# Second layer's experts: weights in 8 KB runs, and four experts as one unit

## The chip, the cores and the metric

One core of a Trainium2 chip runs the whole program. The metric is the device time of one execution in microseconds (us). TensorE (PE) does the matmuls, with its weight loads shown apart (PEld); VectorE (DVE), ScalarE (ACT) and GpSimd (POOL) work beside it; SyncE (SP) issues nearly all transfers from memory (HBM) into the on-chip buffer, which 16 DMA engines carry out.

## The reference, cut to what matters

Two layers, each a mixer followed by a mixture of experts. The change touches the second layer's mixture alone, which sees 256 tokens of 1024 floats:

```python
def grouped_moe(h, router_w, router_b, w_gate, w_up, w_down):
    ...   # each token goes to 2 of 16 experts, both in its best group of four
    for e in range(N_EXPERTS):
        hid = jax.nn.silu(h @ w_gate[e]) * (h @ w_up[e])     # 1024 -> 512
        out = out + combine[:, e:e + 1] * (hid @ w_down[e])  # 512 -> 1024
    return out
```

All weights are float32. One expert has three matrices of 2 MiB (gate and up 1024 x 512, down 512 x 1024), so a layer's experts are 96 MiB.

## The kernel before, in words

**Units.** A layer's experts are worked off in units. A unit of one expert ("S") has 128 slots for tokens, a unit of two ("P") 64 slots for each; `PLAN` (L24) gives the order, for layer two `PPSPSPPPP`. Experts 0 to 4 stand at fixed places (units 0 to 2), so that their weights can be loaded before the routing is known. The others are sorted by their number of tokens (`order`): the fullest is the later S, the next ones fill the pairs from the fullest down, so the emptiest four are the last two pairs. Their numbers reach SyncE as register values (`expert`, L293). If an expert has more tokens than slots, a fallback (`overflow`) runs all experts for the tokens that found no slot.

**One unit.** Its token numbers come from a comparison of ranks (`slots1`), GpSimd gathers the token rows (`gather1`, three units ahead), TensorE transposes them in 8 blocks of 128 x 128 (`xpose1`, L1628) so that the features lie on partitions, block k holding features 128k to 128k+127. `gu` computes gate and up with the tokens as weight operand and the experts' matrices streamed past them. `hidden` makes silu(gate) x up x routing weight, `hid_T` transposes it in 4 blocks, `down` multiplies with the down matrix, first the left half of the output, then the right half, and splits each half into a high and a low part. `combine1` adds the result to the tokens' rows by a one-hot matmul. In program order these stand as gate n+1, down n, up n+1, combine n; a scheduler orders each engine's instructions at build time from its own model of durations.

**Matmuls.** `mm_unit` (L906) goes through the four blocks of a tile. For an S unit each product is three float32r matmuls of high and low parts (`mm3`), whose parts ScalarE, VectorE and GpSimd make per tile. For a P unit each expert's matmul is plain float32 on half of TensorE's columns (64), the two experts one after the other for each block; in the profile a float32 matmul stands as two records.

**Weights.** `Stream` (L95) holds the list of all weight tiles of the program in the order of use: for layer two gate 0, up 0, gate 1, down 0, up 1, and so on (`add_moe`, L301). A tile is 128 partitions x 4 x 512 floats, 1 MiB. A free buffer is filled with the next tile of the list by SyncE (`load`, L127); when the last matmul of a tile is issued, its buffer is released and the next load goes behind it. In layer two there are 12 buffers: `RING` = 7, `EXTRA` = 4, and one made of two separate halves (`Two`), which takes two transfers. Every tile is read as 512 rows x 512 columns, row 128k + p on partition p at place k: each partition gets four runs of 512 floats, 2 KB each. For the down matrix a tile is a column half.

**The end.** The last unit's down has its own code: product, weighting, one-hot matmul, addition and the squares for the final norm for the left half, then for the right half; then the test for overflow, the norm and two output transfers of 512 KB.

Of the kernel before, what the change touches and what calls it, by code (L numbers as in the profile page):

```python
# [10 lines left out]
F32 = mybir.dt.float32  # L11
# [3 lines left out]
OP = mybir.AluOpType  # L15
AX = mybir.AxisListType

D = 1024
KD = 8
NE = 16  # L20
EPS = 1e-6
NEG = -1.0e30
OFF = 4096.0
PLAN = ("SSSPSSSPSSSPS", "PPSPSPPPP")  # L24
FIXED = (2, 5)

RING, NPIECE = 7, 4
# [11 lines left out]

C_TRI, C_ONE, C_IOR, C_END = 0, 128, 256, 384  # L40

C_IOP, C_IDT, C_RK, C_THR, C_IO2, C_EID, C_KBE, C_KB, C_CAP, C_SEL, C_SEND = 0, 1, 5, 9, 13, 14, 15, 17, 49, 81, 97


def units_of(l):

    plan, fixed = PLAN[l], FIXED[l]
    units, p = [], 0
    while p < fixed:
        n = 1 + (plan[len(units)] == "P")  # L50
        units.append(tuple(range(p, p + n)))
        p += n
    rest = plan[len(units):]
    solo, pairs = iter(range(p, NE)), iter(range(p + rest.count("S"), NE, 2))
    for x in rest:
        if x == "S":
            units.append((next(solo),))
        else:
            p = next(pairs)
            units.append((p, p + 1))  # L60
    return units


# [35 lines left out]
class Stream:  # L99
# [28 lines left out]
    def load(self):  # L128
        while self.free and self.loaded < min(len(self.src), self.limit):
            i = self.loaded  # L130
            self.owner[i] = self.free.pop(0)
            t = self.owner[i][0]()
            for dst, src in self.src[i]:
                src = src() if callable(src) else src
                if isinstance(t, Two):
                    for j in range(2):
                        self.nc.sync.dma_start(t.t[j], src[:, 2 * j:2 * j + 2])
                elif i in self.behind:
                    with self.tc.issue_after(self.behind[i].ins):
                        self.nc.gpsimd.dma_start(dst(t), src)  # L140
                else:
                    self.nc.sync.dma_start(dst(t), src)
            self.tiles[i] = t
            self.loaded += 1
# [63 lines left out]
def backbone(ctx: ExitStack, tc: tile.TileContext, I, out):  # L208
# [16 lines left out]
    def y_t():  # L225
        return psum.tile([128, 512], F32, name="yp", tag="yp", bufs=2)
# [5 lines left out]
    st = Stream(tc, ring, RING, NPIECE)  # L232
# [67 lines left out]
    def add_moe(l):  # L300
        def src(w, p, r0, c0):  # L301
            return [(lambda t: t, lambda: w[expert(l, p), r0:r0 + 512, c0:c0 + 512].rearrange(
                "a (k p) f -> (a p) k f", p=128))]

        def put(name, w, u, pos):
            for r0, c0 in pos:
                for p in u:
                    st.add((name, l, p), src(w, p, r0, c0), len(u) == 1)

        wg, wu, wd = (I[n][l] for n in ("moe_w_gate", "moe_w_up", "moe_w_down"))  # L310
        rows2, cols2 = ((0, 0), (512, 0)), ((0, 0), (0, 512))
        for n, u in enumerate(UNITS[l]):
            put("g", wg, u, rows2)
            if n:
                put("d", wd, UNITS[l][n - 1], cols2)
            put("u", wu, u, rows2)
        put("d", wd, UNITS[l][-1], cols2)

    add_moe(0)
    for p in ADA_ODD[:NPRE]:  # L320
# [52 lines left out]
    rk4 = csm[:, C_RK:C_RK + 4]  # L373
    thr = csm[:, C_THR:C_THR + 4]
    iop2 = csm[:, C_IO2:C_IO2 + 1]
    eid = csm[:, C_EID:C_EID + 1]
    kbe = [csm[0:16, C_KBE + l:C_KBE + l + 1] for l in range(2)]
    kb = [csm[0:16, C_KB + 16 * l:C_KB + 16 * l + 16] for l in range(2)]
# [528 lines left out]
    def mm_unit(o, l, n, name, xh, xl, s, first, last, between=()):  # L907

        u = UNITS[l][n]
        w = [st.take((name, l, p)) for p in u]  # L910
        i = st.taken - len(u)
        for k in range(4):
            kk = s * 4 + k
            if len(u) == 1:
                mm3(o, xh[:, kk], xl[:, kk], w[0].h(k), w[0].l(k), first and k == 0, last and k == 3)
            else:
                for h in range(2):
                    hs = slice(h * 64, h * 64 + 64)
                    T.matmul(o[hs], xh[:, kk, hs].bitcast(F32), w[h][:, k], start=first and k == 0, stop=last and k == 3,  # L919
                             skip_group_check=True)  # L920
            if k == 1 and len(u) == 1:
                st.half()
            if k == 3:
                for h in range(len(u)):
                    st.done(i + h)
            if k % 2:
                for f in between[k // 2:k // 2 + 1]:
                    f()

    def gu(name, l, n, xh, xl, at={}):  # L930
# [6 lines left out]
            mm_unit(pp, l, n, name, xh, xl, s, s == 0, s == 1, [run(at.get(s * 2 + j, ())) for j in range(2)])  # L937
        return pp

    def down(pool, l, n, hh, hl, yh, yl):  # L940
        for half in range(2):
            pp = y_t()
            mm_unit(pp, l, n, "d", hh, hl, 0, True, True)
            hs = slice(half * 512, half * 512 + 512)
            split(yh[:, hs], yl[:, hs], pp, V)

    def order(l, pool, nch, oh):

# [50 lines left out]
    def spread_ranks(u, rT, n):  # L999

        m = 128 // len(u)
        pb = tr_t()
        if len(u) == 1:
            T.matmul(pb[:, 0:n], idr[:, u[0]:u[0] + 1].to_broadcast([16, 128]), rT, start=True, stop=True)
        else:
            for h in range(2):
                T.matmul(pb[h * m:h * m + m, 0:n], idt[0:16, u[h]:u[h] + 1].to_broadcast([16, m]), rT.bitcast(F32),
                         start=True, stop=True, skip_group_check=True)
        return pb[:, 0:n], iop if len(u) == 1 else iop2

    def hidden(pool, pg, pu, w):
        sg = pool.tile([128, 512], F32, name="sg", tag="sg", bufs=2)
# [1 line left out]
        V.scalar_tensor_tensor(sg, sg, w, pu, op0=OP.mult, op1=OP.mult)  # L1014
        return sg

    def hid_T(pool, hid, pair):
        pt = tr_t()
        for q in range(4):
            T.transpose(pt[:, q * 128:(q + 1) * 128], hid[:, q * 128:(q + 1) * 128], idt)  # L1020
        hh = pool.tile([128, 4, 128], F32R, name="hh", tag="hh", bufs=1)
        if pair:
            V.tensor_copy(hh.bitcast(F32).rearrange("p k t -> p (k t)"), pt)  # L1023
            return hh, None
        hl = pool.tile([128, 4, 128], F32R, name="hl", tag="hl", bufs=1)
        p4 = pt.rearrange("p (k t) -> p k t", k=4)
        S.activation(hh, p4, AF.Copy)
        V.tensor_sub(hl, p4, hh.bitcast(F32))
        return hh, hl
# [550 lines left out]
    with phase("moe1") as mp:  # L1580
# [18 lines left out]
        def slots1(n):  # L1599

            u = units[n]
            w = 128 // len(u)
            sg = mp.tile([128, 2, 128], F32, name="sgm", tag="sgm", bufs=2)
            for c in range(2):
                for h, p in enumerate(u):
                    V.tensor_scalar(sg[:, c, h * w:h * w + w], ior[:, 0:w], ranks[:, c, p:p + 1], None, op0=OP.is_equal)
            pw_ = tr_t()
            m = 2 * len(u)
            for c in range(2):
                T.matmul(pw_[:, 0:m], sg[:, c], idw[:, c, u[0]:u[0] + len(u)].rearrange("p e j -> p (e j)"),  # L1610
                         start=(c == 0), stop=(c == 1))
            V.tensor_scalar(sli[0:w, n:n + 1], pw_[0:w, 1:2], OFF, None, op0=OP.add)
            if len(u) == 2:
                V.tensor_scalar(sli[w:128, n:n + 1], pw_[w:128, 3:4], OFF, None, op0=OP.add)
            t = mp.tile([128, 1], F32, name="slw1", tag="slw1", bufs=4)
            for h in range(len(u)):
                hs = slice(h * w, h * w + w)
                V.tensor_copy(t[hs], pw_[hs, 2 * h:2 * h + 1])
            slw[n] = t
            return sg  # L1620
# [7 lines left out]
        def xpose1(n, sg=None):  # L1628
# [3 lines left out]
            for hf in range(2):  # L1632
                pt = tr_t()
                for q in range(4):
                    ks = slice((hf * 4 + q) * 128, (hf * 4 + q) * 128 + 128)
                    o = pt[:, q * 128:(q + 1) * 128]
                    if sg is None:
                        T.transpose(o, xg[n][:, ks], idt)
                    else:
                        for c in range(2):  # L1640
                            T.matmul(o, f1[c][:, ks], sg[:, c], start=(c == 0), stop=(c == 1))
                fs = slice(hf * 4, hf * 4 + 4)
                if xl is None:
                    (V.tensor_copy if hf else S.copy)(xh[:, fs].bitcast(F32).rearrange("p k t -> p (k t)"), pt)
                else:
                    split(xh[:, fs], xl[:, fs], pt.rearrange("p (k t) -> p k t", k=4), V)
# [38 lines left out]
        reg = any_over(mp, over)  # L1685
        for n in range(NU):
            if n:
                down1(n - 1, *hid_T(mp, hid, len(units[n - 1]) == 2))
            pu = gu("u", 1, n, *xT[n])
            hid = hidden(mp, pg, pu, slw[n])  # L1690
            slotsT1(n)
# [6 lines left out]
                    gather1(n + 3)  # L1698
                pg = gu("g", 1, n + 1, *xT[n + 1])

        hh, hl = hid_T(mp, hid, len(units[-1]) == 2)
        gfb = mp.tile([128, D], F32, name="gfb", tag="xl", bufs=1)
        Q.dma_start(gfb, I["final_g"].partition_broadcast(128))
        yb = x_t("yb", "Y")
# [35 lines left out]
def constants():  # L1740
# [14 lines left out]
    small[:, C_RK:C_RK + 4] = 4 - np.arange(4)  # L1755
    small[:, C_THR:C_THR + 4] = 2 - np.arange(4)
    small[:, C_IO2] = p % 64 + 1
    small[:, C_EID] = p
    e = np.arange(NE)
    for l in range(2):  # L1760
# [62 lines left out]
```

## Time and profile before

| | |
|---|---|
| median of 3 runs | 1020.47 us (1019.87 to 1021.63) |
| the profiled execution | 1022.2 us |
| its span, first to last instruction | 1020.4 us |
| TensorE busy, mean granted clock | 943.5 us (92%), 0.963 |
| DVE, ACT, POOL busy | 538.9, 342.2, 351.0 us |
| HBM read | 295.97 MB, 294 GB/s over the span |

The profile is of one execution. Times in its rows count from the first instruction. "Busy" is the union of an engine's instructions; a matmul's end is modelled. A bracket behind an instruction is the engine's idle time before it and what ended that.

### The profile page before, as it was taken

What the parts mean: (1) busy time and instruction counts of PE and PEld (TensorE: products, weight loads), DVE (VectorE), ACT (ScalarE), POOL (GpSimd) and SP (SyncE); (2) the same over time, 40 slices, a digit from 0 to 9 for tenths busy, and PEclk for the clock granted to TensorE, in tenths of its full rate; (3) what the DMA queues carried; (4) which work ended last, traced back from release to release, by engine and by line L of the source; (5) the groups of instructions that cost most, each with busy time, mean ns of one, the idle gap of its engine ahead of it and who ended that gap; (6) DMA issues with size and microseconds to landing.
All of it is one profiled execution on the core that took longest, in us unless ns stands there. A gap on an engine that the chain in (4) does not pass through costs nothing. (4 is left out here: it accounts for less than half of the span.)

```text
span 1020.4 us, 12766 instructions
## 1 busy us (share of the span) xinstructions
PE 943.5 (92%) x4686; PEld 589.3 (58%) x4686; DVE 538.9 (53%) x931; ACT 342.2 (34%) x492; POOL 351.0 (34%) x244
## 2 busy tenths in 40 slices
PE   4999999988899999999999798999796999999995
PEld 2677677746675678558756577466553444643331
DVE  3552425286783777457935683648523464532223
ACT  3421113144563266236534362433201132410001
POOL 2351103235552746524823533023001242443112
PEclk9999999998899999999999999899985999999998
DMA  9964668948699799799599772495496899999993
GB/s 311 363 241 145 213 254 296 350 166 291 217 320 375 248 344 356 251 359 387 203 385 384 255 266 86 123 335 182 157 346 250 326 387 383 387 382 386 386 386 130
DMA packets 149316, 296.28 MB, mean 290 GB/s; under 512 B 6776, under 2 KB 17032, under 8 KB 149112
## 3 DMA queue, kind: packets, MB, share of 16 engines
q1 hardware_dynamic: 143080, 278.06, 76.3%
q0 software_dynamic: 6128, 17.26, 4.6%
q8 instruction: 40, 0.66, 0.3%
q14 instruction: 36, 0.29, 0.1%
q10 hardware_dynamic: 32, 0.01, 0.0%
HBM read 295.97 MB, written 4.24 MB: 294 GB/s over the span
## 5 line engine op out<-in xcount | busy, mean ns | idle before, releaser
L171 ACT ACTIVATE whi<-w 128x1024 fp32r<-128x1024 f32 x182 | 190.6, 1058 | 225.8 <-PE mm L506 93.2
L175 POOL TENSOR_TENSOR wlo<-w,whi 128x1024 fp32r<-128x1024 f32 x64 | 163.5, 2555 | 260.7 <-ACT whi L171 218.4
L175 DVE TENSOR_TENSOR wlo<-w,whi 128x1024 fp32r<-128x1024 f32 x118 | 178.4, 1524 | 95.8 <-ACT whi L171 94.9
L919 PE MATMUL mm<-w,xh 128*64 128x512 f32 x632 | 162.9, 607 | 0.5 <-DMA w<-in_moe_w_up_dram 0.5
L515 POOL TENSOR_TENSOR H<-H,am 128x512 f32<-128x512 f32 x68 | 95.6, 1423 | 146.9 <-DVE am L514 144.5
L919 PEld LDWEIGHTS mm<-w,xh 128*64 128x64 f32 x632 | 48.7, 139 | 90.9 <-issue 87.4
L504 PE MATMUL mm<-whi,xh 128*128 128x512 f32 x192 | 79.6, 414 | 2.4 <-DVE am L514 1.6
L505 PE MATMUL mm<-wlo,xh 128*128 128x512 f32 x192 | 78.8, 410 | 2.7 <-DVE wlo L175 2.3
L506 PE MATMUL mm<-whi,xl 128*128 128x512 f32 x192 | 78.0, 406 | 0.0
L919 PE MATMUL yp<-w,hh 128*64 128x512 f32 x288 | 74.0, 606 | 0.8 <-DVE hh L1023 0.8
L514 DVE TENSOR_TENSOR am<-mm,m5b 128x512 f32<-128x512 f32 x68 | 45.7, 684 | 30.6 <-PE mm L1221 19.5
L1221 PE MATMUL mm<-y,seT 128*128 128x512 f32 x208 | 54.5, 397 | 0.2 <-ACT y L509 0.2
L504 PE MATMUL mm<-aTh,whi 128*128 128x512 f32 x128 | 52.4, 416 | 2.1 <-ACT aTh L665 2.1
L505 PE MATMUL mm<-aTl,whi 128*128 128x512 f32 x128 | 51.7, 404 | 0.0
L506 PE MATMUL mm<-aTh,wlo 128*128 128x512 f32 x128 | 51.3, 402 | 0.0
L1221 PEld LDWEIGHTS mm<-y,seT 128*128 128x128 f32 x208 | 38.1, 188 | 15.4 <-issue 4.9
L919 PEld LDWEIGHTS yp<-w,hh 128*64 128x64 f32 x288 | 23.0, 140 | 41.0 <-issue 39.4
L504 PEld LDWEIGHTS mm<-whi,xh 128*128 128x128 f32 x192 | 37.4, 195 | 14.6 <-issue 4.7
L505 PEld LDWEIGHTS mm<-wlo,xh 128*128 128x128 f32 x192 | 37.5, 195 | 14.4 <-DVE wlo L175 3.4
L432 PE MATMUL yp<-w,sT 128*32 128x512 f32 x288 | 45.2, 642 | 0.0
L506 PEld LDWEIGHTS mm<-whi,xl 128*128 128x128 f32 x192 | 37.5, 195 | 7.8 <-DVE xl L510 0.3
L510 DVE TENSOR_TENSOR yl<-yp,yh 128x512 fp32r<-128x512 f32 x16 | 11.0, 690 | 58.4 <-ACT yh L509 58.4
(362 smaller groups left out, 1546.3 us busy)
## 6 DMA issues: line engine op xcount, KB each, us to landing
w<-in_moe_w_gate_dram SPq DMA_DIRECT2D x61, 1024.0 KB
w<-in_moe_w_up_dram SPq DMA_DIRECT2D x58, 1024.0 KB
w<-in_moe_w_down_dram SPq DMA_DIRECT2D x57, 1024.0 KB
w<-in_ada_w_dram SPq DMA_DIRECT2D x48, 1024.0 KB
w<-in_even_w_in_dram SPq DMA_DIRECT2D x8, 1024.0 KB
w<-in_odd_w_in_dram SPq DMA_DIRECT2D x5, 1024.0 KB
w<-in_even_w_out_dram SPq DMA_DIRECT2D x4, 1024.0 KB
s4b<-mrow SPq DMA_DIRECT2D x6, 512.0 KB
```

The source lines that it names most:

```text
L171: self.nc.scalar.activation(hi, t, AF.Copy)
L175: eng.tensor_sub(lo, t, hi.bitcast(F32))
L432: T.matmul(pa[32 * j:32 * j + 32, :], s_at(s * 4 + j, u), t[:, j, :], start=first and s == 0, stop=last and s == 1, skip_group_check=True)
L504: T.matmul(o, lh, rh, start=first, stop=False)
L505: T.matmul(o, lh, rl, start=False, stop=False)
L506: T.matmul(o, ll, rh, start=False, stop=last)
L510: eng.tensor_sub(lo, x, hi.bitcast(F32))
L514: V.tensor_mul(t, pp, m)
L515: eng.tensor_add(acc, acc, t)
L919: T.matmul(o[hs], xh[:, kk, hs].bitcast(F32), w[h][:, k], start=first and k == 0, stop=last and k == 3, skip_group_check=True)
L1221: marks["comb"] = T.matmul(pp, seT[n][:, c * 128:(c + 1) * 128], t[:, hs], start=(i == 0), stop=(i == 2 * len(ns) - 1))
```

## The change

Three things change, all in layer two (`l == 1`); layer one keeps its tiles, its units and its order.

1. A tile of gate or up holds rows 8p + 4s to 8p + 4s + 3 on partition p (s = 0 or 1), a tile of down rows 4p + 2s and 4p + 2s + 1 in full: 2048 floats that lie together in memory, a run of 8 KB a partition. The last unit's down keeps its column halves. A load into the buffer of two halves takes 4 KB runs.
2. So that tokens and hidden values meet these rows, the transposes read every eighth feature of the tokens (a step of 32 bytes) and every fourth of the hidden product (16 bytes). `down` takes both output halves from each tile, so it accumulates in its two banks side by side (`mm_down`).
3. The plan becomes `PPSPSPPQ`: the last two pairs are one unit "Q" of four experts with 32 slots each, on a quarter of TensorE's columns each.

```diff
-PLAN = ("SSSPSSSPSSSPS", "PPSPSPPPP")
+PLAN = ("SSSPSSSPSSSPS", "PPSPSPPQ")
+
+WIDE = {"S": 1, "P": 2, "Q": 4}
...
+                        if len(src.shape) == 2:
+                            self.nc.sync.dma_start(t.t[j].rearrange("p k f -> p (k f)"), src[:, 1024 * j:1024 * j + 1024])
+                        else:
+                            self.nc.sync.dma_start(t.t[j], src[:, 2 * j:2 * j + 2])
...
+        def rows_of(w, p, s):
+
+            return [(flat, lambda: w[expert(l, p)].rearrange("a (p s j) f -> s (a p) (j f)", p=128, s=2)[s])]
...
-                    st.add((name, l, p), src(w, p, r0, c0), len(u) == 1)
+                    st.add((name, l, p), src(w, p, r0, c0) if l == 0 or last else rows_of(w, p, s), len(u) == 1)
...
-        put("d", wd, UNITS[l][-1], cols2)
+        put("d", wd, UNITS[l][-1], cols2, True)
...
-                for h in range(2):
-                    hs = slice(h * 64, h * 64 + 64)
+                m = 128 // len(u)
+                for h in range(len(u)):
+                    hs = slice(h * m, h * m + m)
...
+    def mm_down(os, l, n, hh, hl, s):
+
+        u = UNITS[l][n]
+        w = [st.take(("d", l, p)) for p in u]
+        i = st.taken - len(u)
+        for k in range(4):
+            j, o = 2 * s + k // 2, os[k % 2]
+            if len(u) == 1:
+                mm3(o, hh[:, j], hl[:, j], w[0].h(k), w[0].l(k), j == 0, j == 3)
+            else:
+                m = 128 // len(u)
+                for h in range(len(u)):
+                    hs = slice(h * m, h * m + m)
+                    T.matmul(o[hs], hh[:, j, hs].bitcast(F32), w[h][:, k], start=j == 0, stop=j == 3,
+                             skip_group_check=True)
...
     def down(pool, l, n, hh, hl, yh, yl):
+        os = [y_t(), y_t()]
+        if l:
+            for s in range(2):
+                mm_down(os, l, n, hh, hl, s)
         for half in range(2):
-            pp = y_t()
-            mm_unit(pp, l, n, "d", hh, hl, 0, True, True)
             hs = slice(half * 512, half * 512 + 512)
-            split(yh[:, hs], yl[:, hs], pp, V)
+            if not l:
+                mm_unit(os[half], l, n, "d", hh, hl, 0, True, True)
+            split(yh[:, hs], yl[:, hs], os[half], V)
...
-            T.transpose(pt[:, q * 128:(q + 1) * 128], hid[:, q * 128:(q + 1) * 128], idt)
+
+            T.transpose(pt[:, q * 128:(q + 1) * 128], hid[:, q:512:4] if rows else hid[:, q * 128:(q + 1) * 128], idt)
...
-                    ks = slice((hf * 4 + q) * 128, (hf * 4 + q) * 128 + 128)
+
+                    ks = slice(hf * 4 + q, D, 8)
```

## Rows read from the trace of the kernel before

**Rows 1.** The page: span, busy time, transfer rate in 40 slices, packets.
```profile
span 1020.4 us, 12766 instructions
...
PE 943.5 (92%) x4686; PEld 589.3 (58%) x4686; DVE 538.9 (53%) x931; ACT 342.2 (34%) x492; POOL 351.0 (34%) x244
...
GB/s 311 363 241 145 213 254 296 350 166 291 217 320 375 248 344 356 251 359 387 203 385 384 255 266 86 123 335 182 157 346 250 326 387 383 387 382 386 386 386 130
DMA packets 149316, 296.28 MB, mean 290 GB/s; under 512 B 6776, under 2 KB 17032, under 8 KB 149112
```
**Rows 2.** Stretches of 20 us in layer two's experts, columns in the first line.
```profile
core 0: us, PE busy (x) PEld busy (x) DVE busy (x) ACT busy (x) POOL busy (x), PEclk, DMA share, GB/s
...
780.00:800.00 20.00, 17.61 (x68) 6.57 (x70) 7.52 (x13) 4.94 (x6) 3.35 (x2) 0.78 0.48 171
...
820.00:840.00 20.00, 18.43 (x81) 9.88 (x83) 11.75 (x17) 8.02 (x9) 5.54 (x4) 0.91 1.05 388
840.00:860.00 20.00, 20.00 (x91) 9.15 (x88) 7.05 (x12) 3.57 (x5) 5.57 (x5) 1.00 1.05 388
...
1000.00:1020.00 20.00, 10.04 (x38) 3.37 (x34) 6.84 (x10) 4.04 (x9) 5.10 (x5) 0.85 0.17 68
```
**Rows 3.** Waits of TensorE, 783 to 1003 us: us in total, times, longest.
```profile
PE mm L505 <- DVE wlo L175: 2.3, 1, 2.3
...
PE tr L1638 <- DVE hh L1023: 0.2, 1, 0.2
```
**Rows 4.** Timeline of SyncE's last weight issues: start, us, what, how many.
```profile
968.90 10.27 SPq L142 DMA_DIRECT2D w<-in_moe_w_up_dram  x4
979.41 11.85 SPq L142 DMA_DIRECT2D w<-in_moe_w_down_dram  x4
```
**Rows 5.** Timeline of the end: last down, last scaling of the output.
```profile
999.32 7.09 PE L919 MATMUL yp<-w,hh 128*64 128x512 f32 x32 [0.78 <-DVE hh L1023]
...
1015.57 1.15 ACT L1734 ACTIVATE hg<-hg,rs 128x1024 f32<-128x1024 f32 x1 [3.91 <-POOL rs L1732]
```
**Rows 6.** Two longer stretches of layer two's experts.
```profile
801.70:944.40 142.70, 137.93 (x619) 70.13 (x617) 68.57 (x104) 35.72 (x47) 54.52 (x36) 0.98 1.04 385
944.40:1000.80 56.40, 53.48 (x244) 19.08 (x244) 13.87 (x21) 4.26 (x8) 9.96 (x8) 1.00 1.04 384
```
**Rows 7.** A stretch in which the pooling bands' 8 KB rows are loaded.
```profile
591.50:592.50 1.00, 1.00 (x9) 0.95 (x10) 0.19 (x2) 1.00 (x2) 0.90 (x1) 1.00 1.00 426
```
**Rows 8.** Timeline of TensorE in a pair's down.
```profile
984.12 0.59 PE L919 MATMUL yp<-w,hh 128*64 128x512 f32 x1
984.13 0.59 PE L919 MATMUL yp<-wa,hh 128*64 128x512 f32 x1
984.55 0.59 PE L919 MATMUL yp<-w,hh 128*64 128x512 f32 x1
```
**Rows 9.** Timeline of TensorE, matmuls on 32 columns (the modulation's).
```profile
707.04 1.07 PE L432 MATMUL mm<-w,sT 128*32 128x512 f32 x8
```
**Rows 10.** Timeline of VectorE: hidden products of units 1, 6, 7, 8.
```profile
801.70 0.75 DVE L1014 SCALAR_TENSOR_TENSOR sg<-sg,slw,mm 128x512 f32<-128x512 f32 x1 [4.68 <-PE mm L919]
...
944.37 0.75 DVE L1014 SCALAR_TENSOR_TENSOR sg<-sg,slw,mm 128x512 f32<-128x512 f32 x1 [2.86 <-PE mm L919]
...
971.38 0.75 DVE L1014 SCALAR_TENSOR_TENSOR sg<-sg,slw,mm 128x512 f32<-128x512 f32 x1 [4.52 <-PE mm L919]
...
997.08 0.75 DVE L1014 SCALAR_TENSOR_TENSOR sg<-sg,slw,mm 128x512 f32<-128x512 f32 x1 [4.50 <-PE mm L919]
```
**Rows 11.** Timeline of TensorE: unit 7's token transposes and gate.
```profile
946.61 1.10 PE L1638 MATMUL tr<-idt,xg 128*128 128x128 f32 x8 [0.21 <-DVE hh L1023]
947.64 6.65 PE L919 MATMUL mm<-w,xh 128*64 128x512 f32 x29
```
**Rows 12.** Weight loads of transposes by line: ns min/median/max, first and last start.
```profile
L1638 PEld LDWEIGHTS tr<-idt,xg x64: 138/140/229, 777.5 to 947.3; 128*128 128x128 f32 x64
...
L480 PEld LDWEIGHTS tr<-idt,mcol x7: 85/88/102, 161.6 to 736.1; 128*8 128x8 f32 x4, 128*24 128x24 f32 x2, 128*16 128x16 f32 x1
```

## What the change does to the time, predicted

> **What bounds the kernel now.** I read the page first, then the table of stretches, then the waits of TensorE and the issues of SyncE, last the timeline of the end. The page shows TensorE busy for 92% of the span, and in the strip the transfers flat at 382 to 388 GB/s over the last slices but one [rows 1]. The stretches place this: in 780 to 800 us the transfers move 171 GB/s, between 800 and 1000 us DMA stands at its ceiling, and in the last one the transfers stop while some 20 us of work remain [rows 2]. That last stretch moves 68 GB/s x 20 us = 1.36 MB; two output writes of 0.52 MB are 1.05 of it, so 0.31 MB of weights are left at 1000 us and the last ones land near 1000.8 us.
>
> TensorE looks no less full. Between 783 and 1003 us its waits, seven rows from 2.3 down to 0.2 us, sum to 7.4 us, and none is for a transfer [rows 3]. So the matmuls are never late for weights, yet SyncE's late issues last 2.6 to 3 us each, which is the time of one tile: its queue is full [rows 4]. Both resources end together: DMA at 1000.8, the last down projection from 999.3 to 1006.4, and 14.0 us of combination, norm and output to 1020.4 [rows 5]. To shorten one alone gains nothing: a change has to shorten both, and this one touches both.
>
> **The change, part by part.** A tile is 1 MiB (1.049 MB); layer two has 16 x 6 = 96 tiles; the ring holds 7 + 4 + 1 = 12.
>
> *Runs of 8 KB.* Now a tile arrives in 2 KB runs at 385 GB/s [rows 6], 2.71 us at 387. Of 149,316 packets all but some 200 are under 8 KB [rows 1]; the exception on this queue is one transfer with 8 KB rows (the pooling bands), and a stretch that holds it alone moves 426 GB/s at DMA share 1.00, where 2 KB runs move 388 at 1.05 [rows 7]. Per tile that is 2.46 us. The bounds are 2.71 (runs don't matter, the stretch is too short to count) and 2.35 (426 scaled to share 1.05); I take 2.46. The Trainium skill, "DMA: Bandwidth & Descriptors", section Specifications, puts the smallest transfer at line rate at 512 bytes; by that, 2 KB is already there and the tile stays at 2.71, a rival below. The two levels in rows 2 and 7 speak against it, though over only 1 us. The last unit's down weights (8 tiles) keep 2 KB runs: 2.71 each.
>
> *One unit of four.* TensorE starts the two matmuls of a pair 0.01 us apart and the next two 0.42 later [rows 8], so a step costs 0.425 us whether it holds one half or both. With 32 columns four go together: eight records in 1.07 us are two steps [rows 9]. A pair has 32 steps in gate and up, 16 in down; the unit of four has the same 48. It therefore costs about what one pair does, and one pair unit goes: hidden to hidden 27.0 and 25.7 us for the last two [rows 10], some 26 us of TensorE with its transposes and combination.
>
> *Down by rows.* The two halves of the output are now accumulated side by side in both banks instead of one after the other. Steps and weight loads stay the same in number. Both splits (0.6 us ACT, 0.7 us DVE) come at the end, in front of the next up projection's 6.8 us, which hides them; without that cover 1.3 us a unit. Zero taken.
>
> *Strided transposes.* Twelve a unit (8 of tokens, 4 of hidden) now read every eighth or every fourth float as the weight operand. Contiguous ones load in 0.140 us; the only strided one, every second float, 8 to 24 columns wide, takes 0.085 to 0.102 [rows 12], and says little on a step of 32 bytes. Lower bound zero (the word size is the same), upper a second reading of 0.14 us each, 1.7 us a unit. By the nearest row, which shows no surcharge beyond its columns, I take zero. The Trainium skill, "SBUF — State Buffer", on its 16-byte cachelines, says that each access which crosses to a new line pays; here every element would. No run here shows that price; what it would do is a rival.
>
> *SyncE and queues.* The count of weight issues is the same (96 tiles), each with a quarter of the pieces, so no issue gets longer; one gather on POOL's queue goes. Vector slot work of one unit goes (off the path, zero).
>
> **The sum.** Units 0 to 6 keep their experts and step counts, and TensorE paces them, so unit 6's hidden product stays at 944.4 [rows 10]. By then 68 tiles are consumed (g and u of units 0 to 6, d of 0 to 5). Before, (1000.8 - 944.4) x 384 GB/s = 20.7 tiles were missing, so 75.3 had landed: 7 ahead [rows 6]. The faster rate over the 142.7 us from 801.7 adds (426 - 385) x 142.7 / 1.049 = 5.6 tiles, to 12.9 ahead. The ring allows 12: at 944.4 it is full, with 16 to 17 tiles to come.
>
> If DMA never paused, 9 x 2.46 + 8 x 2.71 = 43.8 us, the end is 988.2. If it waits until the first four tiles of the last gate are released (947.6 [rows 11] + 8 steps = 951.0) plus about 1 us, 8 x 2.46 + 8 x 2.71 = 41.4 gives 993.4. I take 991. Before that, tile 88 (the last of up) lands at 991 - 8 x 2.71 = 969.3; up ends at 972.7, hidden and its transposes take about the 2.2 us seen before, 997.1 to 999.3 [rows 5, 10]; so TensorE then waits for down's tiles, the first wait for weights in this stage. Half 0 comes at 980, half 1 at 991. Its 8 steps and the last one's drain are 3.6 us at full clock. In the stretch with the wait of 2.3 us the granted clock averaged 0.91 [rows 2, 3]; with idle times of several us I expect the 1.2 GHz level in part: 3.6 to 7.0, taken as 5.3, so 996.3. The tail of 14.0 follows: 1010.3. (First-half combination may move ahead of the last matmuls, -1.8; at 1.2 GHz it costs +1.7: they cancel.) That is 10.1 us under the span. The profiled execution took 1022.2 for a span of 1020.4; it stands 1.7 above the median of the three runs, 1020.47, so the median becomes **1010.4**. With the bounds (988.2 + 3.6 + 12.2 and 994.4 + 7.0 + 15.7) its own range is 1004 to 1017.
>
> **Rivals.**
> *A. The runs give nothing* (slower or same). DMA stays at 387 GB/s and still ends at 1000.8, whatever TensorE saves. For it: the evidence for 426 is one stretch of 1 us. Then TensorE idles in the last unit, and 3.6 to 7.0 + 14.0 us follow: 1018.4 to 1021.8 in span, plus the lost prefetch if four tiles released at once let the queue run dry (2 to 4 us): 1019 to 1026.
> *B. The strided reads cost* (slower). Place: 12 weight loads in each of seven units that TensorE paces, 84 in all. Price: x each, added straight to 944.4, after which the last unit follows as before. At 0.12 us each (0.14 becoming 0.26) the 10 us are gone; at twice that the median is 1030. For it: TensorE has no slack between 801.7 and 944.4 (137.9 of 142.7 us busy [rows 6]). Against: a transpose starts every 0.14 us with its load beside the one before (8 in 1.10 us [rows 11]), and each load would have to double.
> *C. The ring starves.* Releases in fours out of twelve leave eight in flight; if each of the last unit's four groups costs 2 us of empty queue on top, DMA ends near 998 and the median is 1017. For it: today already SyncE waits for releases; against: only 8 tiles are left to issue by then.
> *D. Overflow runs.* Were one of the four emptiest experts over 32 tokens, the fallback would stream 2 x 16 x 6 MiB = 201 MB, 500 us more. The reference's routing of its own inputs gives these four 25, 20, 19 and 12 tokens in layer two, so it does not happen.
>
> **How the numbers follow.** Forecast 0.60 (1004 to 1017), C 0.13, A 0.13 (a third of it within the bound of no change, the rest slower), B 0.13 (a fifth faster, a fifth same, the rest slower), D 0.01. About 0.2% either way (2 us, 1018.4 to 1022.5) is what a measurement of this kernel can tell from no change. Faster: 0.60 + 0.13 + 0.03 = 0.76, less 0.02 for C's far end, 0.74; same 0.08; slower 0.18. The range 1002 to 1022 leaves out most of B and part of A.
>
> **What would show it.** Right: 420 GB/s or more in stretches before 944 where the ring has room; LDWEIGHTS of the transposes at 0.14 us; four 32-column matmuls every 0.43 us; hidden of unit 6 within 2 us of 944.4; TensorE waiting for down weights between 975 and 991; last weights landing near 991 and the span's end 19 us behind. Wrong: 388 GB/s again (A), longer transpose loads and a later unit 6 (B), SyncE waiting for releases with DMA idle after 950 (C), or a new order of instructions that moves units 1 to 6.

## The result, and the profile after

The changed kernel takes 1012.33 us (median of 5 runs, 1008.57 to 1013.69) against 1020.47 for the kernel before in its 5; the ratio is 0.9906 with a 95% interval of 0.9884 to 0.9928. The forecast was 1010.4, faster with 0.74; the time lies in its range, 1.9 us above the point. A second timing, beside the experiments, gave 1012.27 and 0.9914 (0.9889 to 0.9939). The profiled execution took 1012.91 us for a span of 1011.1.

The page of the kernel after, its counterpart of [rows 1]:

```profile
span 1011.1 us, 12687 instructions
...
PE 927.9 (92%) x4662; PEld 583.7 (58%) x4662; DVE 532.2 (53%) x921; ACT 340.3 (34%) x488; POOL 346.5 (34%) x239
...
GB/s 316 363 266 125 230 252 290 352 167 299 214 321 374 245 344 362 264 340 387 219 363 385 292 237 84 94 308 237 191 232 326 293 418 407 370 384 419 420 397 132
DMA packets 116276, 296.28 MB, mean 293 GB/s; under 512 B 6632, under 2 KB 16888, under 8 KB 105704
```

TensorE is busy for 15.6 us less, and the rate's flat stretch of 382 to 388 is gone: it is 418 to 420 in three slices, but 370 and 384 in two between them. The table of stretches (as [rows 2]) places those:

```profile
780.00:800.00 20.00, 19.58 (x80) 8.26 (x80) 7.53 (x13) 4.91 (x6) 3.36 (x2) 0.84 0.50 181
800.00:840.00 40.00, 37.70 (x172) 21.59 (x173) 25.00 (x35) 13.15 (x16) 14.79 (x10) 0.96 1.02 420
840.00:860.00 20.00, 20.00 (x92) 9.86 (x89) 7.56 (x15) 4.92 (x7) 4.79 (x5) 1.00 0.95 393
860.00:880.00 20.00, 18.67 (x86) 10.76 (x84) 14.38 (x18) 7.54 (x10) 11.22 (x7) 1.00 0.96 366
880.00:900.00 20.00, 19.57 (x91) 10.15 (x91) 10.56 (x20) 6.33 (x9) 12.64 (x7) 1.00 0.96 397
...
960.00:980.00 20.00, 14.36 (x71) 4.29 (x69) 3.71 (x6) 0.00 (x0) 4.98 (x4) 0.83 1.03 401
```

In 800 to 840 the transfers run at 420 GB/s; from 840 to 900 they lose (27 + 54 + 23) x 20 us = 2.1 MB against that, two tiles or 5 us. In 960 to 980 TensorE is busy for 14.4 of 20 us at a granted clock of 0.83: it waits now. Its waits between 783 and 1000 us (as [rows 3]: what waited, for what, us in total, times, longest):

```profile
PE mm L933 <- DMA w<-in_moe_w_up_dram: 4.1, 2, 2.7
PE yp L933 <- SPq L1130: 3.5, 2, 2.2
PE mm L518 <- DVE wlo L180: 2.3, 1, 2.3
...
PE yp L933 <- DMA w<-in_moe_w_down_dram: 1.0, 1, 1.0
```

Before, no wait in this stage was for a transfer. Now up waits for weights for 4.1 us and down for 1.0 and 3.5 (the line named, L1130, is in the fallback, which does not run here; what is late at 988 and 993 is a tile of down). The waits and the last steps in the timeline of TensorE (start, duration, instruction, how many, idle time before):

```profile
947.36 0.59 PE L933 MATMUL mm<-wa,xh 128*32 128x512 f32 x1
947.36 0.61 PE L933 MATMUL mm<-w,xh 128*32 128x512 f32 x3
947.78 0.59 PE L933 MATMUL mm<-wa,xh 128*32 128x512 f32 x1
947.79 0.60 PE L933 MATMUL mm<-w,xh 128*32 128x512 f32 x3
...
971.54 1.07 PE L933 MATMUL mm<-w,xh 128*32 128x512 f32 x3 [2.74 <-DMA w<-in_moe_w_up_dram]
...
972.39 1.07 PE L933 MATMUL mm<-w,xh 128*32 128x512 f32 x3
...
988.36 1.04 PE L933 MATMUL yp<-w,hh 128*32 128x512 f32 x2 [2.17 <-SPq L1130]
...
993.63 3.62 PE L933 MATMUL yp<-w,hh 128*32 128x512 f32 x26 [1.33 <-SPq L1130]
```

At 947.36 four records on 32 columns start together and the next four 0.42 us later, the step of a pair in [rows 8]. At 971.54 the same step takes 0.85 us: after two waits for weights the granted clock is at its lower level, until 977.4. The last burst starts at 993.63, when the last tile is in, and ends at 997.25; 13.85 us of combination, norm and output follow. The hidden products of units 6 and 7 in the timeline of VectorE (as [rows 10]):

```profile
941.79 0.75 DVE L1053 SCALAR_TENSOR_TENSOR sg<-sg,slw,mm 128x512 f32<-128x512 f32 x1 [4.51 <-PE mm L933]
...
978.09 0.75 DVE L1053 SCALAR_TENSOR_TENSOR sg<-sg,slw,mm 128x512 f32<-128x512 f32 x1 [14.29 <-PE mm L933]
```

Unit 6 comes at 941.79 instead of 944.37, 2.6 us earlier. The kernel is now bound by transfers at its end, and the transfers had pauses.

### The profile page after: what moved, and what is told of

Its sections match the earlier page's. It is cut to its first block, busy times and chain, and to the rows that moved or that the text cites. A ratio compares the mean times of both kernels' runs of the same rounds, so it can differ in the third digit from the quotient of the medians.

```text
span 1011.1 us, 12687 instructions
## 1 busy us (share of the span) xinstructions
PE 927.9 (92%) x4662; PEld 583.7 (58%) x4662; DVE 532.2 (53%) x921; ACT 340.3 (34%) x488; POOL 346.5 (34%) x239
## 5 line engine op out<-in xcount | busy, mean ns | idle before, releaser
L180 DVE TENSOR_TENSOR wlo<-w,whi 128x1024 fp32r<-128x1024 f32 x118 | 181.1, 1546 | 92.5 <-ACT whi L176 91.8
L933 PE MATMUL mm<-w,xh 128*64 128x512 f32 (+1 forms) x616 | 150.9, 617 | 4.8 <-DMA w<-in_moe_w_up_dram 4.8
L528 POOL TENSOR_TENSOR H<-H,am 128x512 f32<-128x512 f32 x64 | 89.7, 1420 | 125.3 <-DVE am L527 122.9
L933 PEld LDWEIGHTS mm<-w,xh 128*64 128x64 f32 (+1 forms) x616 | 43.8, 135 | 88.4 <-issue 78.1
L527 DVE TENSOR_TENSOR am<-mm,m5b 128x512 f32<-128x512 f32 x64 | 42.9, 684 | 28.7 <-PE mm L1261 19.5
L518 PEld LDWEIGHTS mm<-wlo,xh 128*128 128x128 f32 x192 | 37.4, 195 | 14.4 <-DVE wlo L180 3.4
L517 PE MATMUL yp<-whi,hh 128*128 128x512 f32 x96 | 38.2, 397 | 0.7 <-ACT hh L1067 0.7
L1053 DVE SCALAR_TENSOR_TENSOR sg<-sg,slw,mm 128x512 f32<-128x512 f32 x21 | 15.6, 742 | 43.9 <-PE mm L933 41.1
L518 PE MATMUL yp<-wlo,hh 128*128 128x512 f32 x96 | 38.4, 400 | 0.0
```

Of the source, the lines that this page charges most:

```text
L180: eng.tensor_sub(lo, t, hi.bitcast(F32))
L517: T.matmul(o, lh, rh, start=first, stop=False)
L518: T.matmul(o, lh, rl, start=False, stop=False)
L527: V.tensor_mul(t, pp, m)
L528: eng.tensor_add(acc, acc, t)
```

## The experiments

The theory, T: TensorE and the transfers ended together before, each edit shortens one of the two, and only both together shorten the end; strided reads cost nothing. Each run was timed beside runs of the kernel before on the same chip; ratios are against those. Each expectation says which theory and which rivals it means. The edits are shown cut ("...") to the lines that matter.

**1 and 2. Each edit alone.** The unit of four with 2 KB runs, contiguous transposes and down by halves:

```diff
-                    st.add((name, l, p), src(w, p, r0, c0) if l == 0 or last else rows_of(w, p, s), len(u) == 1)
+                    st.add((name, l, p), src(w, p, r0, c0), len(u) == 1)
...
```

> The unit of four alone: every tile in 2 KB runs again, transposes contiguous, down by column halves. Theory T (both resources bound before; either part alone gains little): transfers stay at 385 to 388 GB/s, the last weights land near 1001 us as before, TensorE waits for weights in the last unit, then 3.6 us of matmuls and 13.9 us of tail: span 1018 to 1021, median within 2 us of before. Rival U (TensorE alone was the bound, transfers had slack): the 26 us that the unit saves show at once, with the transfers of the last unit shown as moving faster or ending earlier than 1001: median 995 to 1005.

1020.29 us, ratio 0.9989 (0.9972 to 1.0006): no difference. And the 8 KB runs without the unit of four:

```diff
-PLAN = ("SSSPSSSPSSSPS", "PPSPSPPQ")
+PLAN = ("SSSPSSSPSSSPS", "PPSPSPPPP")
```

> The 8 KB runs alone: plan PPSPSPPPP as before, with rows-wise tiles, strided transposes and down by rows. Theory T: transfers reach 420 GB/s when a buffer is free, then the ring is full and they pause; TensorE sets the pace with the same units, so hidden products of units 6 to 8 come within 3 us of before (944, 971, 997), the last weights land before TensorE needs them, and the median is 1016 to 1021. Rival V (the transfers alone were the bound): the end moves with the last weights, by 96 tiles x 0.2 us = 10 to 16 us: median 1004 to 1010. Rival B (strided reads cost): slower than before, over 1022.

1019.31 us, 0.998 (0.9964 to 0.9996). The gains, 0.1% and 0.2% alone, are 0.9% together. The stretches of the first show why:

```profile
960.00:980.00 20.00, 14.82 (x56) 3.64 (x52) 3.46 (x5) 0.60 (x1) 4.95 (x4) 0.90 1.05 387
980.00:1000.00 20.00, 14.19 (x70) 3.69 (x70) 2.79 (x4) 0.00 (x0) 0.00 (x0) 0.92 1.04 384
```

DMA is at its old ceiling to the end and its last weights land at about 1002, hardly other than before. What TensorE saves it waits: it idles for 11.0 of these 40 us, at granted clocks of 0.90 and 0.92, and its waits from 783 to 1003 rise from 7.4 to 18.1 us. In the second the transfers end first:

```profile
980.00:1000.00 20.00, 18.24 (x80) 6.47 (x78) 5.50 (x8) 1.19 (x2) 4.98 (x4) 1.00 0.59 218
```

They stop at 992, and TensorE goes on at full clock with 7.5 us of waits, as before; its last hidden product stands at 995.6 where it stood at 997.1. T holds: of two resources that end together, shortening one alone gained 0.1 to 0.2%.

**3. Contiguous transposes in the changed kernel.**

```diff
-                    ks = slice(hf * 4 + q, D, 8)
+                    ks = slice((hf * 4 + q) * 128, (hf * 4 + q) * 128 + 128)
...
```

> As the changed kernel, but tokens and hidden products are transposed in contiguous blocks while the weights stay in rows, so features and weight rows do not belong together and the output is not the reference's; the work is the same in kind and number. It prices the strided reads. Theory T: the weight load of a transpose goes back from 0.19-0.21 us to 0.14, but it lies beside the transpose before it, so eight transposes take 1.10 instead of 1.16 us; unit 6's hidden product within 1 us of 941.8, median the same as the changed kernel, 1011 to 1013.5. Rival B: 84 loads x 0.05 to 0.07 us = 4 to 6 us of TensorE come back, median 1006 to 1008.

1011.61 us, 0.9886 (0.9864 to 0.9908), beside 0.9906 and 0.9914 of the changed kernel: the intervals overlap, so no price is clear of the noise, which would hide 2 or 3 us. The 10 us of rival B are ruled out. Yet the loads are not the same. The changed kernel's transposes (weight loads, ns min/median/max), then this run's:

```profile
L1679 PEld LDWEIGHTS tr<-idt,xg x56: 185/192/226, 780.1 to 924.6; 128*128 128x128 f32 x56
L1060 PEld LDWEIGHTS tr<-idt,sg x32: 138/209/218, 794.3 to 979.2; 128*128 128x128 f32 x32
```
```profile
L1679 PEld LDWEIGHTS tr<-idt,xg x56: 138/141/231, 777.5 to 923.8; 128*128 128x128 f32 x56
```

A load takes 192 ns (steps of 32 bytes) or 209 (16 bytes) instead of 141. Eight transposes in a row (at 923.8 us) took 1.16 us against 1.09 in this run, so of the 8 x 0.05 us most passes beside the transpose before it.

**4. Runs of 4 KB** (two runs a partition; tokens then in steps of 8 bytes, hidden values contiguous).

```diff
-            return [(flat, lambda: w[expert(l, p)].rearrange("a (p s j) f -> s (a p) (j f)", p=128, s=2)[s])]
+            if w.shape[-1] == 512:
+                return [(pairs, lambda: w[expert(l, p)].rearrange("a (s i p j) f -> s (a p) i (j f)", p=128, s=2, i=2)[s])]
+            return [(pairs, lambda: w[expert(l, p)].rearrange("a (s i p) f -> s (a p) i f", p=128, s=2)[s])]
...
```

> The changed kernel with runs of 4 KB: gate and up tiles hold two neighbouring rows a partition twice (transposes at a step of 8 bytes), down tiles one full row twice (contiguous transposes of the hidden product). If a run costs a fixed time beside its bytes (2 KB 86 ns, 4 KB 159 ns and 8 KB 309 ns are the medians of single packets before the change: 28 bytes a ns plus 12 ns each), two thirds of the gain are there at 4 KB: 408 to 412 GB/s, last weights near 995, median 1013 to 1015. If the rate grows with the length of the run: 397 to 400 GB/s, last weights near 998 and 1016 to 1018.

1013.16 us, 0.9926 (0.9905 to 0.9946). Its stretches:

```profile
800.00:840.00 40.00, 37.72 (x173) 21.37 (x171) 25.44 (x38) 13.14 (x16) 15.77 (x11) 0.96 1.03 409
...
970.00:985.00 15.00, 9.46 (x48) 2.19 (x52) 1.44 (x2) 0.00 (x0) 0.00 (x0) 0.84 1.05 387
```

The weight loads of its tokens' transposes:

```profile
L1685 PEld LDWEIGHTS tr<-idt,xg x56: 194/209/231, 778.0 to 923.3; 128*128 128x128 f32 x56
```

387 GB/s with 2 KB (the last unit's down in this very run), 409 with 4 KB, 420 with 8 KB: rival A (of the prediction) falls, and two thirds of the gain in rate come with the first doubling. The time hardly differs from the changed kernel's, so the rate alone does not set it. Steps of 8 bytes load in 209 ns.

**5. The last unit's down in 8 KB runs too**, its halves side by side.

```diff
-                    st.add((name, l, p), src(w, p, r0, c0) if l == 0 or last else rows_of(w, p, s), len(u) == 1)
+                    st.add((name, l, p), src(w, p, r0, c0) if l == 0 else rows_of(w, p, s), len(u) == 1)
...
```

> The changed kernel with the last unit's down in 8 KB runs too, both halves of the output accumulated side by side. Theory T: the 8 tiles take 8 x 0.2 = 1.7 us less, so the last weights land near 991.4, but both halves now end together: the first half's scaling, one-hot matmuls, additions and squares, which in the changed kernel lie before the last weights, come behind them, 2 to 3 us: median 1012 to 1015. Rival (that work is hidden behind other engines anyway): 1010 to 1011.

1010.04 us, 0.9896 (0.987 to 0.9923), better than theory T and in the rival's range; so it was run again beside the changed kernel:

> The changed kernel itself, beside the others on the same chip: 1010 to 1013.

> The changed kernel with the last unit's down in 8 KB runs, once more beside the changed kernel. In its first run the last weights landed at 990.4 (2.7 us before the changed kernel's) and the tail behind the last matmul was 14.5 instead of 13.9 us, because the first half's work behind the last weights overlaps the second half's. If that holds: 1.5 to 2 us under the changed kernel's median. If it was noise: within 1 us of it.

1012.27 (0.9914, 0.9889 to 0.9939) and 1012.39 (0.9908, 0.9882 to 0.9934). No difference between the two versions is clear of the noise. The landing at 990.4 tells nothing either: the changed kernel's own two profiles have 993.1 and 990.8, and the profile of the repetition, of its slowest execution (1016.71 us), some 996.

**6 to 8. Another place for the unit of four or for the single experts**, to find what the pauses belong to. The unit of four fourth in the order:

```diff
-PLAN = ("SSSPSSSPSSSPS", "PPSPSPPQ")
+PLAN = ("SSSPSSSPSSSPS", "PPSQSPPP")
```

> The changed kernel with the unit of four between the two single-expert units (PPSQSPPP instead of PPSPSPPQ). Theory T: in the changed kernel the transfers pause after each single-expert unit because the ring is full (241 to 330 GB/s at 855-865 and 895-905, some 6 us lost) and TensorE then waits for weights in the last unit. With the unit of four early, TensorE empties the ring there, transfers run at 420 GB/s from 795 us to the end, the last unit is a pair with only 4 tiles in 2 KB runs: last weights near 988 us, median 1006 to 1009. Rival C' (the end is set by the unit's own burst, not by pauses): the same 24 tiles are missed in the middle, TensorE waits there and is late afterwards; median 1012 to 1017.

1012.37 us, 0.9903 (0.9885 to 0.9922): no gain over the changed kernel, though the last weights landed at 989.6, near the forecast; the median is in the range of rival C'. The missing time is in TensorE: 23 us instead of 18 lie behind the last weights. Between 866 and 920 us it waits 6.6 us for parts of the single experts' tiles, which come too late, and 2.4 us for a tile of down. Of its waits from 783 us on (2.3 us of the first row lie earlier, and stand in the changed kernel as well):

```profile
PE mm L518 <- DVE wlo L180: 3.1, 2, 2.3
...
PE yp L518 <- POOL wlo L180: 1.7, 1, 1.7
...
PE yp L517 <- ACT whi L176: 1.6, 1, 1.6
```

The unit of four sixth, `PPSPSQPP`:

> The changed kernel with the unit of four right after the second single-expert unit (PPSPSQPP), so that both single-expert units still have a full ring ahead of them. Theory T: the pause at 855-865 stays, the one at 895-905 shrinks by about half (1 us), 4 instead of 8 tiles come in 2 KB runs (0.8 us), and the last unit, a pair, is met with few tiles ahead, so the transfers still set the end: last weights 990 to 992, median 1009 to 1012. Rival (TensorE sets the end when a pair comes last, as with the unit of four early, 23 us from the last weights to the end): median 1013 or more.

1020.12 us, 0.9982 (0.9964 to 1.0): the gain is gone, and theory T's forecast with it; the time is in the rival's range, but the last weights land at about 999, some 8 us later than T had them, so the transfers were late too. And six experts at fixed places, the single ones later, `PPPSPSPQ`:

> The changed kernel with the fixed experts 0 to 5 as three pairs and the plan PPPSPSPQ, so that both single-expert units come one place later, after the pairs have used up the lead of the transfers. Theory T (the transfers set the end and lose some 6 us to pauses at 855-865 and 895-905, when the ring is full behind the single-expert units): the pauses shrink, TensorE keeps a lead of loaded tiles in front of each single-expert unit, last weights 988 to 990, median 1007 to 1010. Rival S (a single-expert unit met with few tiles ahead waits for the high and low parts of its weights, as in the run with the unit of four early, where TensorE waited 14.6 us and the median stayed at 1012.4): the pauses go but TensorE's waits take their place, median 1011 to 1015.

1023.31 us, 1.002 (1.0005 to 1.0036): 0.2% slower than the kernel before, outside both ranges. Runs 7 and 8 have longer pauses of the transfers, at 895 to 908 us. Stretches of run 8, then its longest wait of SyncE (total, times, longest):

```profile
880.00:900.00 20.00, 17.13 (x67) 8.73 (x67) 12.78 (x21) 5.92 (x8) 8.25 (x6) 0.91 0.75 304
900.00:920.00 20.00, 18.37 (x71) 10.42 (x70) 6.18 (x8) 6.17 (x8) 1.98 (x1) 0.92 0.78 309
```
```profile
SPq L147 <- DVE wlo L180: 48.1, 8, 18.5
```

SyncE stood for 18.5 us at one issue, until VectorE had made the low part of a single expert's tile. SyncE's waits from 800 us in the changed kernel, then the same row of the kernel before:

```profile
SPq L147 <- DVE wlo L180: 36.5, 8, 10.7
...
SPq L147 <- POOL wlo L180: 9.1, 3, 4.4
```
```profile
SPq L142 <- DVE wlo L175: 17.3, 6, 7.0
```

Such waits take 36.5 us now and took 17.3. With the unit of four alone (run 1) they took 14.6 us, with the 8 KB runs alone (run 2) 38.8, so they grow with the faster transfers. A wait of SyncE costs nothing as long as loads issued before it are still moving; it costs where the transfers pause. How that comes about is seen at the pause that begins at 858 us. The timeline of SyncE has the issue, that of ScalarE what it waited for:

```profile
848.09 15.95 SPq L147 DMA_DIRECT2D w<-in_moe_w_gate_dram  x4
```
```profile
848.19 0.60 ACT L1067 ACTIVATE hh<-tr 128x512 fp32r<-128x512 f32 x1
855.70 1.06 ACT L176 ACTIVATE whi<-w 128x1024 fp32r<-128x1024 f32 x1 [6.91 <-PE yp L519]
```

Four gate tiles follow each other in the program's order, and the second goes into the buffer of a single expert's tile. That buffer is free when both halves of the tile are split into parts (`_prep`); there are four places for parts, and the next part (855.70) waits until a matmul on that expert's down tiles, which were split before, has used one. So SyncE stands from 848.7 to 859.4, and then, for the next such buffer, to 863.1.

The other explanation would be a full ring, with TensorE behind. The buffer of two halves (`wa`, `wb`) tells: its last matmul before the pause, the rate in the pause, and SyncE's next issues:

```profile
852.01 0.59 PE L933 MATMUL mm<-wb,xh 128*64 128x512 f32 x1
```
```profile
856.00:858.00 2.00, 2.00 (x11) 1.63 (x10) 1.20 (x1) 1.74 (x2) 0.00 (x0) 1.00 1.00 418
858.00:860.00 2.00, 2.00 (x12) 1.71 (x11) 1.27 (x3) 1.69 (x4) 0.46 (x1) 1.00 0.37 152
```
```profile
863.13 0.91 SPq L147 DMA_DIRECT2D w<-in_moe_w_gate_dram  x2
864.28 0.33 SPq L147 DMA_DIRECT2D w<-in_moe_w_down_dram  x1
864.85 0.45 SPq L140 DMA_DIRECT2D wa<-in_moe_w_down_dram  x1
```

TensorE was done with that buffer at 852.6; its next load was issued at 864.85, in a row of issues some 0.6 us apart. So it stood empty for 12 us, through most of the pause (858 to 866 us), and its load waited behind the one at the head. The second pause is alike: TensorE ended the four gate tiles of a pair at 895.3, and three loads follow one another only from 899.61, when a part is made.

**9. No single experts.** If that is the cause, a kernel without such units has no pauses. First the simplest form, with pairs in place of the single experts and the fallback's limit raised, which leaves one token out:

```diff
-PLAN = ("SSSPSSSPSSSPS", "PPSPSPPQ")
+PLAN = ("SSSPSSSPSSSPS", "PPPPPPQ")
...
-FIXED = (2, 5)
+FIXED = (2, 6)
...
-                small[:, C_CAP + NE * l + i] = 128 // len(u)
+                small[:, C_CAP + NE * l + i] = 128 // len(u) if l == 0 else 128
```

> The changed kernel without single-expert units: six fixed experts and the next six in pairs, then the unit of four (PPPPPPQ), and no overflow test trips, so one token beyond the 64th of the fullest expert is left out of the output. In the changed kernel SyncE, which fills buffers in order, waits at 848 to 859 and 885 to 899 for the low part of a single-expert unit's tile (VectorE, L180); the matmuls whose four slots for such parts are taken end only then. Theory T (the remaining pauses come from the single-expert units' weight parts, and DMA sets the end otherwise): no pause between 800 and 980 us, transfers at 415 to 420 GB/s throughout, last weights 984 to 988, TensorE waiting for weights in most units, median 1003 to 1007. Rival R (the ring of 12 is simply full because TensorE is behind): pauses of the same 5 to 7 us stay in some pair units; last weights 990 or later, median 1009 to 1012.

1001.12 us, 0.9806 (0.9779 to 0.9832), better than expected. From 800 us on not one of SyncE's waits is for a part, and in the stretch of the pauses the transfers never pause:

```profile
840.00:905.00 65.00, 63.29 (x290) 24.34 (x290) 16.12 (x31) 5.94 (x10) 10.97 (x9) 1.00 1.01 419
```

**10. The whole computation without single experts.** The fullest expert and the emptiest form a unit "R": three quarters of TensorE's columns for the one, all three with the same expert's matrices, and one quarter for the other.

```diff
-PLAN = ("SSSPSSSPSSSPS", "PPSPSPPQ")
+PLAN = ("SSSPSSSPSSSPS", "PPPRPPQ")
...
+def blocks(u):
+
+    if len(u) == 2 and u[1] > u[0] + 1:
+        return [(h, slice(32 * q, 32 * q + 32)) for q, h in enumerate((0, 0, 0, 1))]
+    m = 128 // len(u)
+    return [(h, slice(h * m, h * m + m)) for h in range(len(u))]
...
-FIXED = (2, 5)
+FIXED = (2, 6)
...
-                m = 128 // len(u)
-                for h in range(len(u)):
-                    hs = slice(h * m, h * m + m)
+                for h, hs in blocks(u):
```

(`slots1` and the limits of the fallback follow the same division of the columns.)

> The changed kernel with no single-expert unit and nothing left out: the fullest of the experts that were alone becomes a unit with the emptiest one, as three quarters of 32 columns that share its weights beside one quarter of the other (96 and 32 slots); order of the units: three pairs, this unit, two pairs, the unit of four. Theory T (the parts of a single expert's tiles come late and SP, which fills buffers in the program's order, stands behind them): as in the run without single-expert units, transfers at 419 to 420 GB/s from 800 to 950 us with no slice under 400, last weights at 980 to 984 us, median 1000 to 1004 us, ratio about 0.98. Rival: quarters that share their weights cost TensorE more than a pair (steps over 0.45 us), or a wait of the same kind stays elsewhere: 1005 to 1012 us.

**1000.1 us, 0.98 (0.9771 to 0.9829): faster than both kernels, and as forecast.** Its stretches ahead of those of the second profile of the changed kernel, whose hidden product of the first unit stands at 765.7 us against 764.4 here:

```profile
760.00:800.00 40.00, 31.83 (x141) 13.24 (x139) 10.29 (x45) 1.78 (x4) 3.25 (x3) 0.83 0.77 306
...
840.00:905.00 65.00, 63.52 (x350) 23.34 (x344) 16.00 (x31) 5.76 (x10) 11.01 (x9) 0.97 1.02 419
```
```profile
760.00:800.00 40.00, 31.52 (x139) 13.12 (x139) 14.56 (x43) 6.96 (x8) 5.51 (x4) 0.83 0.73 282
...
840.00:905.00 65.00, 63.22 (x283) 34.72 (x279) 30.32 (x45) 19.22 (x25) 26.79 (x16) 1.00 0.95 380
```

The last weights land at 980.9 instead of 990.8, 9.9 us earlier. Of these, (419 - 380) x 65 us = 2.5 MB or 6.0 us are the pauses, (306 - 282) x 40 = 1.0 MB or 2.3 us the stretch before 800, whose cause was not sought, and 1.3 us the earlier start; such a sum from stretches closes to about 1 us. TensorE still waits for up's weights (4.9 us): the transfers are the bound. Runs 9 and 10 also take work from TensorE (busy 914.1 us in run 10, 927.9 in the changed kernel), which frees buffers sooner, so by themselves they do not separate the parts from a faster TensorE. The timelines of the pauses above do: the buffers were free.

## Why the prediction was right, point by point

- *Both ends move only together*: shown by 1 and 2.
- *Runs of 8 KB, 426 GB/s, 2.46 us a tile*: 420, 2.50 us. The stretch of one microsecond in [rows 7] told the direction and the size, the size in part by luck: it was the fastest of those read there, and the ones of 2 to 3 us around it moved 395 to 403 GB/s (2.60 to 2.65 us a tile). By the Trainium skill, "DMA: Bandwidth & Descriptors", section Specifications, a transfer of 512 bytes reaches line rate; 387, 409 and 420 GB/s for 2, 4 and 8 KB do not agree, and the measurement decides.
- *Unit of four, one pair's steps*: right, 0.42 us for four matmuls.
- *Strided transposes at zero*: right in the time, within the noise (3), wrong in the row: 192 to 209 ns a load, not 140. Most of that is hidden beside the transpose before. Rival B falls.
- *Unit 6 stays at 944.4*: 941.8 and 939.6 in two profiles, 2.6 and 4.8 us earlier where the sign of being right allowed 2; why was not sought.
- *Ring full at 944.4, 16 to 17 tiles to come*: this step failed. From 944.4 to the last weights the transfers never paused (420, then 386 GB/s), which is 23.6 us x 418 + 25 x 387 = 19.5 MB or 18.6 tiles. The sum of 5.6 tiles gained over 142.7 us took the higher rate as if SyncE could always issue; it stood behind a single expert's buffers and over 2 tiles were lost between 840 and 905. Another 0.8 goes with the rate (420, not 426: 4.8 tiles gained). That these waits existed was to be seen in the trace of before, among SyncE's waits (17.3 us for parts); I had not asked what held the buffers at their head. The reading of the late issues [rows 4] as a full queue was wrong as well: between 960 and 1000 us SyncE waited 16.7 us for TensorE to be done with buffers (8.2, 4.4, 2.2 and 1.9 us in four rows of its waits).
- *Last weights at 988.2 to 993.4, taken 991*: 993.1 and 990.8 in two profiles. That 991 was met is luck: it is the middle of two cases that both begin with a full ring at 944.4, and neither occurred. Less the 6.0 us of the pauses the first profile would have 987.
- *Waits for weights only in down, up's end at 972.7*: too simple. Up waited too (4.1 us), and the lower clock fell on its last steps: end 978.1.
- *Last burst 3.6 to 7.0, taken 5.3*: 3.62, at full clock; so the lower clock had been priced in the wrong place. Tail 14.0: 13.85.
- *Span 1010.3*: 1011.1 and 1009.0. In the first profile errors cancel: the last weights are 2.1 us later than taken, the burst starts 0.5 us behind them, and it is 1.7 us shorter. The mechanism (both ends move together, then the transfers set the end) was right; the closeness of the point is in part luck. Rivals A, B and D did not occur; C's starving came, but in the middle of the stage and from another cause than releases in fours.

What stays open: the first run of 5 and its repetition differ by 2.4 us with the same code, so differences under that are not explained here. Why run 7 lost the whole gain, with its last weights at about 999, was followed only to its longer pause. More places for parts, the other way to the same end, was not tried.

## What to carry to other kernels

When two resources end together, price a change of one at next to nothing (0.1 and 0.2% here) and look for the change of the other. A rate gained is worth only what the queue in front of it can issue: with one engine filling buffers in program order, one buffer that comes free late holds up all loads behind it, also those whose buffers are free. The list of that engine's own waits shows such a place before the change is made, though not its price: the waits cost time only once the faster transfers had caught up with them. Moving such a unit to another place moved the wait (6 to 8); taking its kind away removed it (9, 10).

## What was not expected of the hardware

- The rate of transfers into 128 partitions grew with the run: 387, 409, 420 GB/s for 2, 4 and 8 KB, one core at work.
- In the transposes of tokens and hidden values a weight load of 128 float32 columns took 140 ns contiguous, 192 ns in steps of 32 bytes, 209 in steps of 16, and 209 also in steps of 8 (4). (Elsewhere in the same traces contiguous loads of this width take 192 ns as well, as at L1650 of the changed kernel, so 140 is not the price of every contiguous load.) The Trainium skill, "SBUF — State Buffer", section Specifications (TRN2), wants two accesses to each line of 16 bytes for the full rate; steps of 8 bytes have two and steps of 16 have one, and both take 209 ns, so the rows agree that a stride costs, but not with that boundary.
- Four float32 matmuls on 32 columns each go in the time of two on 64, also when three of them read the same expert's matrix (32 records in 3.64 us in the unit of four and in the last run's unit R).
